# The first stage of a two-layer trunk kernel: loads in a set order, shifts by groups of 32 columns, products by arrival

## The chip, the cores and the metric

The kernel runs on one core of one Trainium2 chip. The metric is the time of one execution on the device, in microseconds (us), the median of three runs.

## The reference

The program is a backbone with two layers (DEPTH 2, D_MODEL 1024) over 256 latent tokens `x` and 256 context tokens. Each layer is a SwiGLU FFN, a token mixer with four branches, and a second FFN. Before each of the three, the activations are modulated: multiplied by 1 + scale and shifted, where shift, scale and gate come from the conditioning vector by one large product.

```python
x = x + pos_emb_2d(rows)
mod_x = (silu(c) @ w_ada[l] + b_ada[l]).reshape(..., 3, 3, D_MODEL)   # sub-layer s: shift, scale, gate
def modulate(h, mods, s):
    return h * (1 + mods[..., s, 1, :]) + mods[..., s, 0, :]
def swiglu_ffn(h, w_in, w_out):
    a = h @ w_in
    return (silu(a[..., :D_FF]) * a[..., D_FF:]) @ w_out
x = layer_norm(ALPHA * x + 0.5 * gate * swiglu_ffn(modulate(x, mod_x, 0), ...), ln_g, ln_b)
```

The context tokens take the same path with `c_ctx` in the place of `c`. All is float32. The part that the change touches is the first modulation: `shift` and `scale` of the first sub-layer for the 1024 channels, `x` with its positions, the modulated `x`, and the first products of the first FFN.

## The kernel before

**Layout.** The 256 context and 256 latent tokens stand side by side as 512 columns; the 1024 channels are eight tiles k = 0 to 7 of 128 partitions. A float32 product is made of three faster ones (`mm3`, L156): of each operand the ScalarE (ACT) makes a rounded copy `hi`, the VectorE (DVE) subtracts it to get the rest `lo` (`split`, L127), and the TensorE (PE) adds weight-hi x `xh`, weight-hi x `xl` and weight-lo x `xh`. A weight tile of 128 x 1024 (512 KB) holds 128 output channels for all eight k. It is loaded into a ring of four buffers named `raw` (`wload`, L135), split, and used in 24 products of 512 columns. In the trace all products carry the line of the helper `mm` (L122), all ACT operations that of `act` (L125), and all counted DVE operations that of `counted` (L113).

**The first stage** is `start` (L383). It goes through four groups u = 0 to 3, each with k = 2u and 2u + 1. For a group it orders on SP, the queue of the loads, two `ada` tiles (the scale columns of `w_ada`, 512 KB each, in the same `raw` ring), two tiles of `x` (`ah`) and the four shift weights `shw` of the next group.
- *Shift.* PE makes a row of 256 values from `shw` (`row`, eight products with the two columns of `ccol`), ACT copies the row, PE turns it into columns (`shift`), ACT adds the bias (`bp`).
- *Scale.* The DVE multiplies an `ada` tile with the conditioning vector, broadcast over the partitions (`cbc`), and sums: one operation of 128 x 1024 per k and vector (L421, named `junk` by its unused output). A small one adds the bias (`gp`).
- *Modulated x.* POOL (GpSimd) adds the positions (L430), ACT makes `xf` from `ah`, `gp` and `bp` and rounds it to `xh`, the DVE subtracts to `xl`.

After groups 0, 1 and 2 the function calls `mid`, which loads and splits two weight tiles of the first FFN each: six tiles, thus 6 x 24 = 144 products, that accumulate over k as the `x` tiles arrive (`mmk`).

**What sets the order.** The tile framework's scheduler orders the instructions of each engine around the program order and places the semaphores; a ring buffer is loaded again when its last reader has finished. Behind the first stage, `ffn` runs the 22 pairs of output tiles in three parts, each followed by the products of the second weight. Between tiles, `pump` (L260) takes steps from `bg`, the generators `mods` (L226): the scale, shift and gate values of the later sub-layers, by scalings of 128 x 1024 on the DVE (L235), for which one more `ada` tile is loaded into the `raw` ring every two steps.

```python
c = sp.tile([128, 2080], F32, tag="big", name=nm("cbc"), bufs=1)[:, :2 * D]
nc.sync.dma_start(c[:, q], I["cvec"][q].partition_broadcast(128))
act(hi, src, AF.Copy)
tt(out=lo, in0=src, in1=hi.bitcast(F32), op=ALU.subtract)
```

## Time and profile before

| | |
|---|---|
| median of three runs | 2256.55 us (2255.21 to 2262.13) |
| the profiled execution | 2258.55 us |
| its span in the trace | 2256.8 us |
| its mean granted PE clock | 0.993 |
| instructions in the trace | 30633 |

The span is the time from the first to the last instruction that the trace shows; the execution's own time has a little around it. The rows on which the prediction rests stand in a section of their own, below. In a row of a timeline the first number is the start in the span, the second the duration, the name before `<-` is what is written, those behind it what is read, and the brackets hold how long the engine stood idle before and what ended it. In a row of groups the part behind the first `|` is the busy time of the group and the mean of one instruction in ns, the part behind the second the idle time before them.

### The profile page before, as it was taken

The page shows a single profiled execution, that of the slowest core. Times are in us where ns is not written, and L with a number is a line of the kernel's source. Part 1 is how long each engine was busy: PE and PEld are TensorE (multiplying, and loading weights), DVE is VectorE, ACT ScalarE, POOL GpSimd, SP SyncE. Part 2 cuts the span into 40 slices and gives each one's busy share as a digit, 9 for nine tenths or more (in the row PEclk, how much of TensorE's full clock was granted, in tenths as well). Part 3 has the DMA queues.
Part 4 walks back from the last instruction along what each step waited for, and adds up shares of the span by engine and source line. Part 5 has one row for each costly group of instructions (what it writes and reads, how often), then busy time and mean ns, then how long its engine had stood idle before and what let it go on. Part 6 is the DMA issues. An engine that isn't in the chain of part 4 may idle for free.

```text
span 2256.8 us, 30633 instructions
## 1 busy us (share of the span) xinstructions
PE 2216.5 (98%) x11700; PEld 1880.7 (83%) x11700; DVE 1649.4 (73%) x2947; ACT 959.4 (43%) x1521; POOL 19.4 (1%) x82
## 2 busy tenths in 40 slices
PE   7999999999999999999999999999999999999998
PEld 4888788988888888898888888888889998998887
DVE  6998855768996754795746488766558989767777
ACT  5322223732335743362222244222326645756554
POOL 2000000000000000000000000000000000000000
PEclk9999999999999999999999999999999999999999
DMA  8676642323332132244535425554434643354652
GB/s 309 216 228 220 201 156 92 106 77 121 96 95 83 57 105 92 94 139 151 186 103 168 131 85 187 189 159 163 143 102 137 191 141 109 114 169 143 202 187 85
DMA packets 94452, 323.18 MB, mean 143 GB/s; under 512 B 10592, under 2 KB 12640, under 8 KB 94304
## 3 DMA queue, kind: packets, MB, share of 16 engines
q1 hardware_dynamic: 94304, 321.22, 44.7%
q8 instruction: 92, 1.51, 0.3%
q14 instruction: 56, 0.46, 0.1%
HBM read 320.12 MB, written 1.05 MB: 142 GB/s over the span
## 4 chain that ended last, share of the span: by engine, by line
PE 86%; DVE 6%; DMA 3%; ACT 2%; issue 2%; SPq 0%; DVEq 0%; ACTq 0%
PE mm L122 81%; DVE junk L235 2%; DVE lo L113 1%; DMA ada<-in_wada 1%; PE num L122 1%; DMA raw<-in_ffn_in 1%; DVE junk L421 1%; ACT hi L125 1%; DMA raw<-in_ffn_out 1%; DVE ah L113 1%; PE bcr L122 1%; PE gt L122 0%; PE ax L122 0%; PE qk L122 0%; PE bcm L122 0%
## 5 line engine op out<-in xcount | busy, mean ns | idle before, releaser
L125 ACT ACTIVATE hi<-raw 128x1024 fp32r<-128x1024 f32 (+1 forms) x462 | 473.2, 1030 | 996.0 <-PE mm L122 617.7
L122 PE MATMUL mm<-xh,hi 128*128 128x512 f32 (+1 forms) x2448 | 873.2, 365 | 6.7 <-ACT hi L125 3.6
L122 PE MATMUL mm<-xh,lo 128*128 128x512 f32 (+1 forms) x2448 | 849.2, 347 | 0.0
L122 PE MATMUL mm<-xl,hi 128*128 128x512 f32 (+1 forms) x2096 | 749.3, 358 | 0.4 <-DVE xl L113 0.4
L113 DVE TENSOR_TENSOR lo<-raw,hi 128x1024 fp32r<-128x1024 f32 (+1 forms) x462 | 544.8, 1184 | 234.7 <-ACT hi L125 231.2
L122 PEld LDWEIGHTS mm<-xh,hi 128*128 128x128 f32 x2448 | 460.8, 189 | 83.7 <-ACT hi L125 5.0
L122 PEld LDWEIGHTS mm<-xh,lo 128*128 128x128 f32 x2448 | 463.6, 189 | 58.6 <-DVE lo L113 0.9
L122 PEld LDWEIGHTS mm<-xl,hi 128*128 128x128 f32 x2096 | 396.0, 189 | 58.7 <-DVE xl L113 0.7
L122 PE MATMUL mm<-gh,hi 128*128 128x512 f32 (+1 forms) x1424 | 402.9, 364 | 1.8 <-ACT gh L125 1.2
L235 DVE CUSTOM_DVE_ANT_0 junk<-ada,cbc 128x1024 bf16<-128x1024 f32 x256 | 312.8, 1222 | 100.3 <-DMA ada<-in_wada 97.0
L122 PEld LDWEIGHTS mm<-gh,hi 128*128 128x128 f32 x1424 | 254.5, 188 | 50.7 <-ACT gh L125 1.6
L122 PE MATMUL mm<-gh,lo 128*128 128x512 f32 (+1 forms) x800 | 275.3, 344 | 0.7 <-DVE lo L113 0.7
L122 PEld LDWEIGHTS mm<-gh,lo 128*128 128x128 f32 x800 | 150.4, 188 | 21.4 <-DVE lo L113 1.1
L113 DVE SCALAR_TENSOR_TENSOR ah<-mm,gate,ah 128x256 f32<-128x256 f32 x216 | 95.7, 478 | 90.0 <-PE mm L122 89.6
L113 DVE SCALAR_TENSOR_TENSOR cacc<-pd,cw,cacc 128x512 f32<-128x512 f32 (+1 forms) x240 | 132.9, 609 | 0.2
L122 PE MATMUL mm<-yh,hi 128*128 128x512 f32 (+1 forms) x512 | 129.3, 339 | 0.1
L113 DVE TENSOR_TENSOR sg<-sg,mm 128x512 f32<-128x512 f32 (+1 forms) x87 | 53.6, 616 | 70.5 <-PE mm L122 70.1
L122 PEld LDWEIGHTS mm<-yh,hi 128*128 128x128 f32 x512 | 88.0, 189 | 11.6 <-ACT yh L125 0.3
L125 ACT ACTIVATE gh<-sg 128x512 fp32r<-128x512 f32 (+1 forms) x88 | 50.8, 578 | 89.5 <-DVE sg L113 89.1
L122 PE MATMUL mm<-yh,lo 128*128 128x512 f32 (+1 forms) x256 | 86.5, 338 | 0.0
L122 PE MATMUL mm<-mh,hi 128*128 128x256 f32 (+1 forms) x320 | 67.0, 306 | 0.5 <-ACT mh L125 0.3
L125 ACT ACTIVATE xf<-ah,bp,gp 128x256 f32<-128x256 f32 x88 | 48.7, 592 | 21.6 <-DVE ah L113 15.0
(263 smaller groups left out, 1798.0 us busy)
## 6 DMA issues: line engine op xcount, KB each, us to landing
raw<-in_ffn_in SPq DMA_DIRECT2D x176, 512.0 KB, 3.8
ada<-in_wada SPq DMA_DIRECT2D x136, 512.0 KB, 4.2
raw<-in_ffn_out SPq DMA_DIRECT2D x64, 512.0 KB, 3.6
raw<-in_w_G SPq DMA_DIRECT2D x64, 512.0 KB, 3.5
raw<-in_w_br SPq DMA_DIRECT2D x32, 512.0 KB, 3.5
raw<-in_ffn_out SPq DMA_DIRECT2D x32, 384.0 KB, 3.6
raw<-in_w_o SPq DMA_DIRECT2D x24, 512.0 KB, 3.5
shw<-in_wshift SPq DMA_DIRECT2D x16, 256.0 KB, 5.9
```

The costliest lines, as they stand in the source:

```text
L113: return f(*a, **k)
L122: nc.tensor.matmul(o, w, x, **kw)
L125: S.activation(o, i, f, **kw)
L235: V.tensor_tensor_reduce(out=cur["junk"], in0=w, in1=cur["c"][:, v], scale=1.0, scalar=0.0, op0=ALU.mult, op1=ALU.add, accum_out=m[:, v, t ...
L421: V.tensor_tensor_reduce(out=cur["junk"], in0=w, in1=cur["c"][:, v], scale=1.0, scalar=0.0, op0=ALU.mult, op1=ALU.add, accum_out=m[:, v, k ...
```

## The change

The first stage is written anew, in the program order that each engine is to keep: PE, SP, DVE and ACT take their instructions in the stage exactly as they are written (`manual_schedule`).
- *Loads.* `LOADS` names the order, part by part: `a` scale weights of a k, `x` a tile of x, `s` shift weights of a group, `W` a weight tile, `p` positions. Scale weights come in halves of 512 columns to blocks of the general pool (`blk`), no longer to the `raw` ring. The conditioning vector is loaded as 8 KB, and broadcast by four products on PE.
- *Shift.* The eight products of a group go to four column groups of 32 columns each (`c32`, the two columns of `ccol` and 30 of zeros); the product that makes columns of the row sums the four groups (`pick`). `SHIFTS` says after how many `mm3` of a k the next group stands on PE.
- *Group 2* also makes the scales of k = 4 and 5 on PE (`wmod`, eight blocks of 512 columns), for which the DVE has no scalings any more. The others have four half scalings each (L479).
- *Positions* are added on the DVE.
- *Products.* `TILES` says how many of the six tiles take part at each k. When a k arrives, the tiles that are new first catch up on the earlier k.
- *Behind the stage.* Loads for `mods` wait for the order of the last x load, its scalings stand behind the last `xl`; the weight tiles of j = 3 are loaded and split right behind the stage (`ahead`).

On ACT, around the `hi` of the sixth weight tile, before: `bp`, `gp` are the columns of shift and scale, `ah` the x tile (which is scaled at the end of its use), `wh` the two halves of the `hi` of the fifth and the sixth tile.

```order
L125 ACTIVATE bp_127<-shift_129,cols_99 128x2
L125 ACTIVATE xf_292<-ah_106,bp_127,gp_126 128x256 x2
L125 ACTIVATE bp_127<-shift_129,cols_99 128x2
L125 ACTIVATE xh_118<-xf_292 128x512
L125 ACTIVATE ah_106<-ah_106 128x512
L125 ACTIVATE xf_303<-ah_107,bp_127,gp_126 128x256 x2
L125 ACTIVATE wh_310<-raw_308 128x512
L125 ACTIVATE xh_120<-xf_303 128x512
L125 ACTIVATE wh_311<-raw_308 128x512
L125 ACTIVATE ah_107<-ah_107 128x512
L125 ACTIVATE wh_321<-raw_319 128x512
L125 ACTIVATE wh_322<-raw_319 128x512
```

And now (`hi_417` is the sixth tile's, `row_388` the row of group 2):

```order
L130 ACTIVATE ah_105<-ah_105 128x512
L130 ACTIVATE row_388<-row_387 128x512
L130 ACTIVATE bp_127<-shift_407,cols_99 128x2
L130 ACTIVATE gp_126<-shift_407,b_129 128x2
L130 ACTIVATE bp_127<-shift_407,cols_99 128x2
L130 ACTIVATE gp_126<-shift_407,b_129 128x2
L130 ACTIVATE hi_417<-raw_343 128x1024
L130 ACTIVATE xf_422<-ah_106,bp_127,gp_126 128x256 x2
L130 ACTIVATE xh_118<-xf_422 128x512
L130 ACTIVATE xf_458<-ah_107,bp_127,gp_126 128x256
L130 ACTIVATE ah_106<-ah_106 128x512
L130 ACTIVATE xf_458<-ah_107,bp_127,gp_126 128x256
```

The sixth tile's `hi` stood behind the `xh` of k = 4 and 5; it now stands ahead of the `xf` of k = 4, and behind the row copy and the four small operations that wait for group 2 on PE.

On the DVE, at the scalings of k = 6 and 7, before: `junk` is a scaling, the row behind it reads its sum, `alg` are small operations for later sub-layers.

```order
L421 ISA junk_98,sc_128<-ada_330,cbc_93 128x1024
L421 ISA sc_128 128x1
L113 TENSOR_SCALAR gp_126<-sc_128,cols_99 128x2
L421 ISA junk_98,sc_128<-ada_332,cbc_93 128x1024
L421 ISA sc_128 128x1
L113 TENSOR_SCALAR alg_387<-cols_100 128x8 x2
L421 ISA junk_98,sc_128<-ada_332,cbc_93 128x1024
L421 ISA sc_128 128x1
L113 TENSOR_TENSOR xl_123<-xf_352,xh_122 128x512
L113 TENSOR_SCALAR gp_126<-sc_128,cols_99 128x2
L113 TENSOR_SCALAR alg_390<-cols_100 128x8 x2
```

And now (`xl_121` is that of k = 5, `xl_123` that of k = 6, `ada_358` the scale weights of k = 7):

```order
L118 TENSOR_TENSOR xl_121<-xf_458,xh_120 128x512
L479 ISA junk_147,sc_128<-ada_353,cbc_132 128x512
L479 ISA sc_128 128x1
...
L479 ISA junk_147,sc_128<-ada_354,cbc_132 128x512
L479 ISA sc_128 128x1
L118 SCALAR_TENSOR_TENSOR gp_126<-sc_128,b_129 128x2
L118 TENSOR_TENSOR ah_108<-ah_108,pos 128x256
L118 TENSOR_TENSOR xl_123<-xf_503,xh_122 128x512
L479 ISA junk_147,sc_128<-ada_358,cbc_132 128x512
```

The scalings of k = 6 and 7 all stood ahead of the `xl` of k = 6; now those of k = 6 stand behind the `xl` of k = 5, and those of k = 7 behind the `xl` of k = 6.

```diff
-MID = (0, 1, 2)
+
+LOADS = ("a0 x0 p s0 W0 a1 x1 W1", "s1 a2 x2 W2", "a3 x3 W3", "W4 s2", "x4 x5 W5 s3 a6 x6 a7 x7")
+TILES = (1, 2, 3, 5, 6, 6, 6, 6)
+
+SHIFTS = {1: 2, 3: 8, 5: 3}
...
-    def load_c():
+    def load_c(first=False):
 
         c = sp.tile([128, 2080], F32, tag="big", name=nm("cbc"), bufs=1)[:, :2 * D]
-        for v in range(2):
-            q = slice(v * D, v * D + D)
-            nc.sync.dma_start(c[:, q], I["cvec"][q].partition_broadcast(128))
-            act(c[:, q], c[:, q], AF.Silu)
+        if first:
+            two = wp.tile([128, 1024], F32, tag="raw", name=nm("two"), bufs=4)[0:2]
+            nc.sync.dma_start(two, I["cvec"].rearrange("(v d) -> v d", v=2))
+            for v in range(2):
+                for h in range(2):
+                    p = aux("cb")
+                    mm(p, ident[0:2, v:v + 1].to_broadcast([2, 128]), two[:, h * 512:h * 512 + 512], start=True, stop=True)
+                    act(c[:, v * D + h * 512:v * D + h * 512 + 512], p, AF.Silu)
+        else:
+            for v in range(2):
+                q = slice(v * D, v * D + D)
...
+    c32 = const.tile([128, 8, 32], F32, name="c32")
+    V.memset(c32, 0.0)
+    act(c32[:, :, 0:2], ccol, AF.Silu)
+    pick = const.tile([128, 2], F32, name="pick")
+    tt(out=pick, in0=ident[:, 0:2], in1=ident[:, 32:34], op=ALU.add)
+    for j in (64, 96):
+        tt(out=pick, in0=pick, in1=ident[:, j:j + 2], op=ALU.add)
...
-            nc.sync.dma_start(w, I["wada"][l, s * 24 + t])
+            with tc.issue_after(last["dma"].ins):
+                nc.sync.dma_start(w, I["wada"][l, s * 24 + t])
             for v in range(2):
-                V.tensor_tensor_reduce(out=cur["junk"], in0=w, in1=cur["c"][:, v], scale=1.0, scalar=0.0,
-                                       op0=ALU.mult, op1=ALU.add, accum_out=m[:, v, t:t + 1])
+                with tc.issue_after(last["xl"].ins):
+                    V.tensor_tensor_reduce(out=cur["junk"], in0=w, in1=cur["c"][:, v], scale=1.0, scalar=0.0,
+                                           op0=ALU.mult, op1=ALU.add, accum_out=m[:, v, t:t + 1])
                 yield
...
-    def start(mid):
...
+    def start():
+        m = const.tile([128, 2, 2, 8], F32, name="sc00")
+        b1 = const.tile([128, 8], F32, name="b100")
+        ld, tiles, done, rows = {}, [], [], {}
+        def load(names):
+            for x in names.split():
+                n = int(x[1:] or 0)
+                if x == "p":
+                    nc.sync.dma_start(pos, I["pos"])
+                elif x[0] == "a":
+                    ld[x] = [blk("ada") for _ in range(2)]
+                    for i in range(2):
+                        nc.sync.dma_start(ld[x][i], I["wada"][0, 8 + n, :, i * 512:i * 512 + 512])
+                elif x[0] == "s":
+                    src = [I["wmod"][i] for i in range(8)] if n == 2 else [I["wshift"][min(n, 2), i] for i in range(4)]
+                    ld[x] = [blk("shw") for _ in src]
+                    for t, w in zip(ld[x], src):
+                        nc.sync.dma_start(t, w)
+                elif x[0] == "x":
+                    last["dma"] = nc.sync.dma_start(ah[n], I["xc"][n])
+                else:
+                    raw = wp.tile([128, D], F32, tag="raw", name=nm("raw"), bufs=4)
+                    nc.sync.dma_start(raw, I["ffn_in"][0, 0, n // 2, n % 2])
+                    ld[x] = raw
+        def add(n):
+            hi = wp.tile([128, 1024], F32R, tag="hi", name=nm("hi"), bufs=6)
+            lo = wp.tile([128, 1024], F32R, tag="lo", name=nm("lo"), bufs=6)
+            split(hi, lo, ld["W%d" % n])
+            tiles.append((aux() if n == 5 else mmb(), hi, lo))
+            done.append(0)
+        def products(upto):
+            for k in range(upto + 1):
+                for n in range(TILES[upto]):
+                    if done[n] == k:
+                        p, wh, wl = tiles[n]
+                        mm3(p, ktile(wh, k), ktile(wl, k), xs[k], full, k == 0, k == 7)
+                        done[n] += 1
+                        yield
+        def group(u):
+            r, rs = aux("row"), blk("row")
+            w = ld["s%d" % u]
+            n = 512 if len(w) == 8 else 256
+            for i in range(8):
+                j = 32 * (i % 4)
+                x = w[i] if n == 512 else w[i // 2][:, (i % 2) * 256:(i % 2) * 256 + 256]
+                mm(r[j:j + 32, 0:n], c32[:, i], x, start=i < 4, stop=i >= 4)
+            act(rs[:, :n], r[:, :n], AF.Copy)
+            rows[u] = rs, n
+        def columns(u):
+            rs, n = rows.pop(u)
+            q = aux("shift")
+            for i in range(n // 128):
+                mm(q[:, 2 * i:2 * i + 2], rs[:, i * 128:i * 128 + 128], pick, start=True, stop=True)
             for k in (2 * u, 2 * u + 1):
+                i = 2 * (k % 2)
+                act(b[:, k], q[:, i:i + 2], AF.Identity, bias=col(0, "b_ada", k))
+                if n > 256:
+                    act(g[:, :, k], q[:, 4 + i:6 + i], AF.Identity, bias=b1[:, k:k + 1])
+        def scales(k):
+            for v in range(2):
+                for i, w in enumerate(ld["a%d" % k]):
+                    V.tensor_tensor_reduce(out=cur["junk"][:, :512], in0=w, in1=cur["c"][:, v, i * 512:i * 512 + 512],
+                                           scale=1.0, scalar=0.0, op0=ALU.mult, op1=ALU.add, accum_out=m[:, v, i, k:k + 1])
+            stt(out=g[:, :, k], in0=m[:, :, 0, k], scalar=b1[:, k:k + 1], in1=m[:, :, 1, k], op0=ALU.add, op1=ALU.add)
+        def positions(k):
+            x3 = ah[k][:, T:].rearrange("p (r c) -> p r c", c=64)
+            pk = (pos[:, 4 * k:4 * k + 4].rearrange("p (r c) -> p r c", c=1) if k < 4 else
+                  pos[:, 16 + (k - 4) * 64:80 + (k - 4) * 64].rearrange("p (r c) -> p r c", r=1))
+            tt(out=x3, in0=x3, in1=pk.to_broadcast([128, 4, 64]), op=ALU.add)
+        def modulated(k):
+            xf = blk("xf")
+            for v in range(2):
+                act(xf[:, vcols(v)], ah[k][:, vcols(v)], AF.Identity, scale=g[:, v, k:k + 1], bias=b[:, k, v:v + 1])
+            last["xl"] = split(xs[k].hi, xs[k].lo, xf)
+        ET = mybir.EngineType
+        with tc.manual_schedule(engines={ET.PE, ET.SP, ET.DVE, ET.Activation}):
+            load_c(True)
+            nc.sync.dma_start(cols[0], I["cols"][0])
+            load(LOADS[0])
+            ts(out=b1, in0=col(0, "b_ada", 8, 8), scalar1=1.0, scalar2=None, op0=ALU.add)
+            scales(0)
+            positions(0)
+            group(0)
+            add(0)
+            columns(0)
+            modulated(0)
+            for _ in products(0):
+                pass
+            load(LOADS[1])
+            for k in range(1, 8):
+                if "a%d" % k in ld:
+                    scales(k)
+                positions(k)
+                new = list(range(TILES[k - 1], TILES[k]))
+                for n in new[:1]:
+                    add(n)
+                modulated(k)
+                for n in new[1:]:
+                    add(n)
+                if k < 4:
+                    load(LOADS[k + 1])
+                todo = products(k)
+                if k in SHIFTS:
+                    for _ in range(SHIFTS[k]):
+                        next(todo)
+                    group(k // 2 + 1)
+                    for _ in todo:
+                        pass
+                    columns(k // 2 + 1)
+                for _ in todo:
+                    pass
...
-                wh, wl = wload(I["ffn_in"][l, w, j, h])
+                wh, wl = ahead.pop((l, w, j, h), None) or wload(I["ffn_in"][l, w, j, h])
...
-                elif j == 0:
-                    mmk(tiles, xs, cs)
-                else:
+                elif j:
                     for t in tiles:
                         mmk([t], xs, cs)
+                else:
+                    for h in range(2):
+                        ahead[l, w, len(js), h] = wload(I["ffn_in"][l, w, len(js), h])
...
-    o["wshift"] = a["w_ada"][0, :, :D].reshape(4, 2, 128, 4, 256).transpose(3, 0, 2, 1, 4).reshape(4, 4, 128, 512)
+
+    w0 = a["w_ada"][0]
+    o["wshift"] = np.concatenate([w0[:, :512], w0[:, 768:D]], axis=1
+                                 ).reshape(4, 2, 128, 3, 256).transpose(3, 0, 2, 1, 4).reshape(3, 4, 128, 512)
+    o["wmod"] = np.concatenate([w0[:, 512:768], w0[:, D + 512:D + 768]], axis=1).reshape(8, 128, 512)
```

## Rows read from the trace of the kernel before

**Rows 1.** The page: busy time (share of the span) and instructions of each engine.
```profile
PE 2216.5 (98%) x11700; PEld 1880.7 (83%) x11700; DVE 1649.4 (73%) x2947; ACT 959.4 (43%) x1521; POOL 19.4 (1%) x82
```

**Rows 2.** Windows: length, PE, PEld, DVE, ACT, POOL (instructions), clock, DMA share, GB/s.
```profile
0.00:20.00 20.00, 9.32 (x36) 3.33 (x36) 7.34 (x25) 6.86 (x13) 3.29 (x12) 1.00 0.91 326
20.00:40.00 20.00, 16.14 (x65) 9.51 (x66) 16.61 (x24) 11.41 (x21) 5.68 (x4) 1.00 0.94 339
```

**Rows 3.** Chain of waits, in order of time: start, length, what.
```profile
6.03 6.44 DMA ada<-in_wada
...
76.02 2.29 DVE lo L113 x2
...
234.60 133.62 PE mm L122 x583
```

**Rows 4.** Timeline of PE: the first product, the tiles' end, and the waits.
```profile
22.37 0.50 PE L122 MATMUL mm<-xh,hi 128*128 128x512 f32 x1 [2.55 <-ACT hi L125]
...
68.11 0.39 PE L122 MATMUL ax<-xh,wl 128*128 128x512 f32 x1
68.34 0.39 PE L122 MATMUL mm<-xh,hi 128*128 128x512 f32 x1
...
131.51 0.50 PE L122 MATMUL mm<-gh,lo 128*128 128x512 f32 x1 [0.70 <-DVE lo L113]
...
233.52 0.50 PE L122 MATMUL mm<-gh,hi 128*128 128x512 f32 x1 [1.17 <-ACT gh L125]
234.60 0.50 PE L122 MATMUL mm<-gh,hi 128*128 128x512 f32 x1 [0.57 <-DVE gh L113]
```

**Rows 5.** Timeline of the DVE: the last xl of the stage.
```profile
57.18 0.69 DVE L113 TENSOR_TENSOR xl<-xf,xh 128x512 fp32r<-128x512 f32 x1
```

**Rows 6.** Groups by line and shape, whole span: busy, mean ns | idle before.
```profile
L113 DVE TENSOR_TENSOR lo<-raw,hi 128x1024 fp32r<-128x1024 f32 x422 | 513.3, 1221 | 223.4 <-ACT hi L125 219.9
...
L125 ACT ACTIVATE hi<-raw 128x1024 fp32r<-128x1024 f32 x422 | 445.3, 1060 | 917.7 <-PE mm L122 592.9 <-issue 227.2 <-DMA raw<-in_ffn_in 66.7
...
L235 DVE CUSTOM_DVE_ANT_0 junk<-ada,cbc 128x1024 bf16<-128x1024 f32 x256 | 312.8, 1222 | 100.3 <-DMA ada<-in_wada 97.0
...
L125 ACT ACTIVATE xf<-ah,bp,gp 128x256 f32<-128x256 f32 x88 | 48.7, 592 | 21.6 <-DVE ah L113 15.0 <-DVE gp L113 5.6 <-ACT ah L125 0.9
...
L113 DVE TENSOR_TENSOR ah<-ah,bcm 128x256 f32<-128x256 f32 x80 | 29.9, 409 | 1.6 <-PE bcm L122 1.6
...
L421 DVE CUSTOM_DVE_ANT_0 junk<-ada,cbc 128x1024 bf16<-128x1024 f32 x16 | 22.0, 1375 | 1.2 <-DMA ada<-in_wada 0.9
...
L113 DVE TENSOR_TENSOR xl<-xf,xh 128x512 fp32r<-128x512 f32 x8 | 5.4, 686 | 2.2 <-ACT xh L125 2.2
...
L125 ACT ACTIVATE xh<-xf 128x512 fp32r<-128x512 f32 x8 | 4.9, 620 | 0.1
...
L122 PE MATMUL st<-lns,ones 128*32 128x128 f32 x44 | 4.3, 273 | 0.0
```

**Rows 7.** DMA from 0 to 60 us, in 40 slices of 1.5 us.
```profile
GB/s 0 79 238 314 376 402 384 417 381 391 406 401 418 404 384 356 399 407 374 183 194 270 303 305 377 427 374 229 186 284 308 310 261 107 300 270 172 259 68 292
```

**Rows 8.** Window of the `mm` tiles alone: PE, PEld, DVE, ACT, clock, DMA share, GB/s.
```profile
22.00:36.10 14.10, 7.96 (x28) 4.87 (x29) 0.00 (x0) 0.00 (x0) 1.00 0.90 313
```

**Rows 9.** Timeline of PE: products with few columns of weights.
```profile
16.64 3.18 PE L122 MATMUL row<-shw,ccol 128*2 128x256 f32 x14
...
392.88 0.41 PE L122 MATMUL st<-sq,ones 128*32 128x128 f32 x4
393.12 0.39 PE L122 MATMUL st<-lns,ones 128*32 128x128 f32 x4
```

**Rows 10.** Windows behind the stage, columns as in rows 2.
```profile
57.87:131.45 73.58, 72.93 (x319) 59.36 (x317) 70.38 (x116) 19.87 (x26) 0.00 (x0) 1.00 0.69 214
131.45:234.60 103.15, 101.35 (x444) 83.00 (x444) 91.24 (x146) 31.75 (x38) 0.00 (x0) 1.00 0.72 228
```

**Rows 11.** Groups by line and shape, 0 to 60 us.
```profile
L430 POOL TENSOR_TENSOR ah<-ah,pos 128x256 f32<-128x256 f32 x8 | 11.0, 1392 | 38.0 <-DMA ah<-in_xc 38.0
```

More of the change, by code (lines that the diff above doesn't have):

```diff
@@ L105, in trunk_kernel @@
     work = {"pe": 0.0, "v": 0.0}
+    last = {}
     def size(ap):
@@ L129, in split @@
             act(hi, src, AF.Copy)
-            tt(out=lo, in0=src, in1=hi.bitcast(F32), op=ALU.subtract)
+            return tt(out=lo, in0=src, in1=hi.bitcast(F32), op=ALU.subtract)
         else:
@@ L195, in trunk_kernel @@
     cur = {}
-    def load_c():
+    def load_c(first=False):
         c = sp.tile([128, 2080], F32, tag="big", name=nm("cbc"), bufs=1)[:, :2 * D]
-        for v in range(2):
-            q = slice(v * D, v * D + D)
-            nc.sync.dma_start(c[:, q], I["cvec"][q].partition_broadcast(128))
-            act(c[:, q], c[:, q], AF.Silu)
+        if first:
[9 more added lines that the diff above has]
+                q = slice(v * D, v * D + D)
+                nc.sync.dma_start(c[:, q], I["cvec"][q].partition_broadcast(128))
+                act(c[:, q], c[:, q], AF.Silu)
         cur["c"] = c.rearrange("p (v d) -> p v d", v=2)
@@ L211, in trunk_kernel @@
         act(identr[r], ident[r, r], AF.Copy)
-    act(ccol, ccol, AF.Silu)
-    load_c()
+    c32 = const.tile([128, 8, 32], F32, name="c32")
[5 more added lines that the diff above has]
+        tt(out=pick, in0=pick, in1=ident[:, j:j + 2], op=ALU.add)
     cols = [const.tile([128, NCOL], F32, name=f"cols{l}") for l in range(DEPTH)]
@@ L437, in start @@
-        nc.sync.dma_start(masks, I["masks"].rearrange("d p t -> p d t"))
-        nc.sync.dma_start(cols[1], I["cols"][1])
+        m = const.tile([128, 2, 2, 8], F32, name="sc00")
[21 more added lines that the diff above has]
+                    ld[x] = raw
@@ L439, in start @@
+        with tc.issue_after(last["dma"].ins):
+            nc.sync.dma_start(masks, I["masks"].rearrange("d p t -> p d t"))
+            nc.sync.dma_start(cols[1], I["cols"][1])
         for k in range(8):
@@ L443, in start @@
                 a = const.tile([128, 2, 8], F32, name=f"alg{l}{s}")
-                ts(out=a[:, 0], in0=col(l, "ln_g", s * 8, 8), scalar1=ALPHA, scalar2=None, op0=ALU.mult)
-                ts(out=a[:, 1], in0=col(l, "ln_b", s * 8, 8), scalar1=ALPHA, scalar2=None, op0=ALU.mult)
+                with tc.issue_after(last["xl"].ins):
+                    ts(out=a[:, 0], in0=col(l, "ln_g", s * 8, 8), scalar1=ALPHA, scalar2=None, op0=ALU.mult)
+                    ts(out=a[:, 1], in0=col(l, "ln_b", s * 8, 8), scalar1=ALPHA, scalar2=None, op0=ALU.mult)
                 alg[l, s] = a
@@ L581, in ffn_tiles @@
             for h in range(2):
-                wh, wl = wload(I["ffn_in"][l, w, j, h])
+                wh, wl = ahead.pop((l, w, j, h), None) or wload(I["ffn_in"][l, w, j, h])
                 tiles.append((mmb(), wh, wl))
         return tiles
-    def first_tiles(n):
-        if n < 2:
-            return ffn_tiles(0, 0, (n,))
-        tiles = []
-        for h in range(2):
-            raw = wp.tile([128, D], F32, tag="raw", name=nm("raw"), bufs=4)
-            nc.sync.dma_start(raw, I["ffn_in"][0, 0, n, h])
-            hi, lo = [blk("wh", F32R) for _ in range(2)], [blk("wl", F32R) for _ in range(2)]
-            for i in range(2):
-                split(hi[i], lo[i], raw[:, i * 512:i * 512 + 512])
-            tiles.append((aux() if h else mmb(), hi, lo))
-        return tiles
+    ahead = {}
     def ffn(l, w, bd, first, cs, order, np_, nm_=1):
@@ L1247, in trunk_kernel @@
     order = (1, 0)
-    x0 = start(first_tiles)
+    x0 = start()
     bg += [mgen[0, 0], mgen[0, 1], mgen[0, 2]]
```

45 lines of the change are left out of this document (removed).

## The prediction, made before the changed kernel was run

> **What bounds the kernel now.** I read the table of busy time first: PE is busy 2216.5 of 2256.8 us [rows 1]. Only some 40 us can ever be won by removing PE's waits. The windows then say where they lie: PE is busy 9.32 us of the first 20, 16.14 of the next 20 [rows 2]. So 14.5 us, a third of all idle time, is at the start, where the change works. The chain of waits says what holds it: from 6.03 us it runs through an `ada` load, the DVE's scalings, DVE splits and the loads that these release, and only at 234.60 does it pass to PE for good [rows 3]. Up to there PE is busy but not on the chain. The PE timeline agrees: PE waits 0.70 us at 131.51 for a `lo` of the DVE, and 1.17 and 0.57 us at 233.52 and 234.60 for `gh` [rows 4]. So up to 234.6 PE has no slack against the DVE: what delays the DVE's stream by more than PE itself is delayed comes out at the end. What counts is therefore not when PE starts, but when the DVE finishes the first stage; in the kernel before it ended its last `xl` at 57.87 (57.18 + 0.69) [rows 5].
>
> **The stage, worked out.** Durations [rows 6]: a scaling holds the DVE 1.22 and 0.04 to the next, 1.26; a half one, which the trace doesn't have, is shorter by (1221 - 686) ns, the difference of a DVE split of 1024 and of 512 columns, so 0.72, four per k 2.9 us (bounds: 0.63, half a scaling, and 1.26; I take the nearest form). A split `lo` holds the DVE 1.15, `xl` 0.6, the position add on the DVE 0.41 at most (a 128x256 add), ACT `hi` 1.0, two `xf` 1.1, `xh` 0.62. PE starts a product every 0.23 us (68.11, 68.34) [rows 4].
>
> 1. First product. The first `ada` landed at 12.47 [rows 3] with 2943 KB ordered up to and with it (8, 64, 1024, 1024, 175, 136, 512). In the new order W0 ends at 2695 KB, 248 KB less at some 390 KB per us (the rate reads 356 to 418 GB/s from slice 5 to slice 19 [rows 7]): 11.8. Then `hi` 1.0, `bp`, two `xf` and `xh`: first product at 15.0 instead of 22.37 [rows 4], last split `xl0` done at 15.7. The broadcast by PE costs nothing: four products of 512 columns in the shadow of that load.
> 2. k = 1 to 3. The DVE does four half scalings (2.9), gp and positions (0.5), `lo` (beside it ACT's two `xf` and `xh`, 1.7 with hand-overs 1.9), `xl`: 5.6 us a round. In the second, `hi` stands on ACT behind the row copy and the `bp` of group 1: 2.0 more. `xl3` at 15.0 + 3 x 5.6 + 2.0 = 33.9, `lo4` done at 36.1. PE then has 31 products behind it. The kernel before had 28 at 36.1 [rows 8]: seven us of head start are spent, since a round here takes one k and the old one handled two together.
> 3. k = 4, 5. PE does 19 products (4.4) and then group 2, 16 records of 512 columns. A record of 256 took 0.227 (14 in 3.18), so 7.3 us one after another; the trace's other use of 32-column groups, `st`, has eight records of 128 columns in two groups from 392.88 to 393.51; less the 0.27 that one takes [rows 6] they start in 0.36, 0.05 apart, where half of 0.227 would be serial [rows 9]: about half. I take half, 3.6: 44.3 with a mode change of 0.2. Row copy 0.6, nine products, four `shift`, four small ACT: 47.9. ACT's order now has `hi` of the sixth tile behind these, so it ends at 48.9, `xl4` at 51.3, `xl5` at 53.7. The DVE idled 12.7 us for that `hi`.
> 4. k = 6. The DVE scales 6 at once (to 57.2), but PE must first do 10 products of tile 5 (its `lo` at 50.2), 18 of k = 4 and 9 of k = 5: 58.8. Group 3 at half 1.8, row copy beside 9 products, `shift`, `bp`: 63.8. `xf`, `xh`, `xl`: 66.3. The DVE idled 8.5.
> 5. k = 7. Its scalings stand on the DVE behind that `xl`: 2.9, gp, positions, `xf`, `xh`, `xl`: 71.9. PE's last 18 products end at 75.9, against 68.34 before.
>
> Check from PE alone: 113 products from 36.1 (25.9), groups and shifts 7.3, and waits of 6.7 (sixth tile 2.5, k = 6 2.7, k = 7 1.5) make 76.
>
> **What follows the stage.** The DVE stream behind it is the same up to the order: two `ada` scalings (2.52) were done before 57.87, now none; at the last `lo` of the first output part one scaling fewer stands before it (38 for 39), so 1.26 more to do, and the twelve small alg operations move behind the stage: 12 x 0.15 = 1.8. Shift of that `lo`: 71.9 - 57.87 + 1.26 + 1.8 = 17.1 us. Against it stands the DVE's own idle time from 57.87 to 131.45, 73.58 - 70.38 = 3.2 us [rows 10]; I let it vanish whole, as four loads lie ready when the stage ends. Shift 13.9. PE came only 0.7 too early there and is 7.6 late itself, so it waits the rest, 6.3 and the old 0.7. From 131.45 on both are shifted alike, the order is the same, and the kernel keeps the 13.9.
>
> The early loads of j = 3 save nothing: the DVE, not the loads, is late then. Homes of their own free the stage's loads from waits on the DVE: the last of them, x7, ends at 13703 KB, 11.8 + 11008 / 390 = 40.0, which is 30 us before its split, so this hides and gains nothing. POOL's adds go to the DVE, 8 x 0.41 = 3.3; it gives back 16 x (1375 - 1222) ns = 2.4, the stretching of the first stage's scalings, some of them beside POOL's adds [rows 6]; both are in the rounds. Two k less on the DVE save 4 scalings, 5.0, in the stretch where it idles: nothing.
>
> By the Trainium skill (TensorEngine Tiling (Array Packing), Tiling Modes, Key Properties) different column tiles execute in parallel, up to four of them for 32 columns; by that groups 1, 2 and 3 cost 0.9, 1.8 and 0.9 less than I take, the last `xl` comes at 68.3, the shift is 10.3 and the time 2266.9. The `st` rows have two groups and can't show four.
>
> By the Trainium skill (SBUF — State Buffer, SBUF: two separate sides) a DVE operation with two SBUF inputs and a POOL operation exclude each other for the whole instruction; the eight adds of 1.39 us [rows 11] could then have cost the DVE up to 11 us, and moving them would be worth up to 8. The scalings lost 2.4 in all, so the trace decides for that.
>
> **Sum.** The profiled execution took 2258.55 us, 2.0 above the median of the runs: 2258.55 + 13.9 = 2272.4 in a profile, 2270.4 against 2256.55. Forecast: 2270. Its own range is 2263 to 2274: shift 17.1 where no idle time vanishes, 6.7 where the three groups cost nothing (1.8, 3.6, 1.8).
>
> **Rivals.**
> - The DVE catches up. It is idle 103.15 - 91.24 = 11.9 us more from 131.45 to 234.60 [rows 10]. If its delay is absorbed there and before, PE's own delay is left: 75.9 - 68.34 = 7.6 less the 2.4 of waits that go: 2261.8, with groups that cost nothing some 5 less. For it: the idle time exists, 15 us in all. Against: it waits for loads whose buffers the DVE itself frees, so it moves with the DVE. 0.17.
> - Faster: the hand-overs of steps 3 to 5 don't cost. If PE reaches group 2 while the loads still come and each copy lies beside products, the DVE never idles its 21 us, and the last `xl` comes at 71.9 - 21.2 = 50.7. The shift is then 50.7 - 57.87 + 3.06 - 3.2 = -7.3: 2249. It decides from a last `xl` before 54.8. For it: all loads are there at 40, and PE has 33 us of products. Against: the order on ACT and DVE is fixed as listed. But my steps are sums of single durations, and the hand-overs between engines are their weakest part. 0.19.
> - The groups run one after another: 3.6 and 7.3 us, last `xl` at 80.5, shift 22.5: 2279. Against: the `st` rows. 0.08.
> - The forecast: 0.56.
>
> A measurement of this kernel tells 0.3% (6.8 us) from no change. Slower by more: the forecast less 0.02, the serial groups, and 0.02 of the first rival: 0.64. Within: 0.15 of the first rival, 0.02 of the forecast and 0.03 of the faster case, whose 2249 lies at the bound: 0.20. Faster: 0.16. The range of 2247 to 2279 leaves out the lower part of the faster case, some 0.09, and half of the serial one.
>
> **What would show it.** First product near 15 us; `xl3` near 34; a DVE gap of about 10 us that ends with the sixth tile's `hi`, one of 8 before `xl` of k = 6; the last `xl` past 66; PE waits for `lo` between 80 and 150 us; the chain of waits still on the DVE at 234. It is wrong if the last `xl` ends before 55, or if PE runs without waits from 76 to 230.

## The result and the profile after

The changed kernel took 2270.19 us (median of five runs, 2269.72 to 2275.59), the kernel before 2256.55 on the same chip: a ratio of 1.0067, 95% interval 1.0056 to 1.0078. By the medians it is slower by 13.6 us, by the means, which the ratio follows, by 15.1; the forecast was 2270. The profiled execution took 2269.72 us with a span of 2267.9 (before 2258.55 and 2256.8).

The page first (as [rows 1]), then the windows of the first 40 us (as [rows 2]):

```profile
PE 2221.2 (98%) x11712; PEld 1883.7 (83%) x11712; DVE 1646.8 (73%) x2972; ACT 961.1 (42%) x1523; POOL 8.3 (0%) x74
```
```profile
0.00:20.00 20.00, 12.84 (x33) 5.52 (x33) 10.12 (x36) 9.21 (x17) 0.54 (x10) 1.00 0.87 311
20.00:40.00 20.00, 14.77 (x55) 9.29 (x56) 14.00 (x30) 10.25 (x18) 0.00 (x0) 0.91 1.04 392
```

PE is busy longer in the first 20 us and shorter in the next 20, and the granted clock is below 1 in the second row, which it was not before. Whoever went by busy time would see a gain in these 40 us: 27.6 us of PE for 25.5. Counted by the products of the weight tiles there is none. Windows of the `mm` tiles alone (as in [rows 8]) have 43 records in 40 us before (first row) and 40 now (second row), and the 40 take longer:

```profile
0.00:40.00 40.00, 11.63 (x43) 7.52 (x43) 0.00 (x0) 0.00 (x0) 1.00 0.93 332
0.00:40.00 40.00, 15.43 (x40) 9.49 (x41) 0.00 (x0) 0.00 (x0) 0.96 0.96 352
```

Up to 26 us the changed kernel starts these products every 0.43 us, while the kernel before starts them every 0.23 us from its first ones on (23.66, 23.90, 24.12). The granted clock reads 1.00 there, but 0.43 us is also the pace of the stretches at 0.50 further down:

```profile
17.59 0.63 PE L127 MATMUL mm<-xh,lo 128*128 128x512 f32 x1
18.01 0.63 PE L127 MATMUL mm<-xh,hi 128*128 128x512 f32 x1
```

The loss shows in the DVE's timeline, which answers to [rows 5]: the split of the sixth tile, then the last three `xl`.

```profile
49.42 1.23 DVE L118 TENSOR_TENSOR lo<-raw,hi 128x1024 fp32r<-128x1024 f32 x1 [10.98 <-ACT hi L130]
...
53.42 0.69 DVE L118 TENSOR_TENSOR xl<-xf,xh 128x512 fp32r<-128x512 f32 x1 [1.33 <-ACT xh L130]
...
66.56 0.69 DVE L118 TENSOR_TENSOR xl<-xf,xh 128x512 fp32r<-128x512 f32 x1 [9.05 <-ACT xh L130]
...
72.15 0.69 DVE L118 TENSOR_TENSOR xl<-xf,xh 128x512 fp32r<-128x512 f32 x1 [1.49 <-ACT xh L130]
```

The last `xl` ends at 72.84, 15.0 us after the 57.87 of before, and the two gaps of 10.98 and 9.05 us are the 12.7 and 8.5 that were forecast. PE's timeline, in answer to [rows 4]: its first product, groups 2 and 3, the last of the 144 products, and every wait of 0.1 us or more from there to 260 us.

```profile
16.27 0.79 PE L127 MATMUL mm<-xh,hi 128*128 128x512 f32 x1 [2.14 <-ACT xh L130]
...
42.71 1.93 PE L127 MATMUL row<-shw,c 128*32 128x512 f32 x16
...
60.73 1.07 PE L127 MATMUL row<-shw,c 128*32 128x256 f32 x16
...
76.75 0.39 PE L127 MATMUL ax<-xh,lo 128*128 128x512 f32 x1
...
90.46 0.50 PE L127 MATMUL mm<-xh,hi 128*128 128x512 f32 x1 [2.44 <-ACT hi L130]
...
91.81 0.80 PE L127 MATMUL mm<-xh,lo 128*128 128x512 f32 x1 [0.61 <-DVE lo L118]
...
136.28 0.50 PE L127 MATMUL mm<-gh,lo 128*128 128x512 f32 x1 [0.17 <-DVE lo L118]
145.35 0.73 PE L127 MATMUL mm<-gh,hi 128*128 128x512 f32 x2 [0.83 <-ACT hi L130]
147.81 0.50 PE L127 MATMUL mm<-gh,lo 128*128 128x512 f32 x1 [1.73 <-DVE lo L118]
152.92 0.51 PE L127 MATMUL mm<-xh,lo 128*128 128x512 f32 x1 [0.53 <-DVE lo L118]
```

The last product starts at 76.75 for 68.11, 8.64 late; the waits behind it sum to 6.31 for the 2.44 of before. In the chain of waits PE takes over for good behind the last of them, at 152.92 and not at 234.60 [rows 3]:

```profile
152.92 230.38 PE mm L127 x1008
```

One thing was in no step of the forecast. Windows of the profile (columns as in [rows 2]) show stretches in which PE ran at a granted clock of 0.50, which is 1.2 GHz, each beginning near a wait; the kernel before has none between its first product and 392 us. Three of the four are shown, the other lies at 29.9 to 33.2 us.

```profile
50.40:53.80 3.40, 3.10 (x7) 2.49 (x8) 1.66 (x4) 3.29 (x6) 0.00 (x0) 0.50 0.49 154
...
67.40:70.80 3.40, 3.40 (x8) 2.63 (x9) 3.11 (x10) 0.44 (x1) 0.00 (x0) 0.50 0.02 5
91.30:94.70 3.40, 2.89 (x7) 2.32 (x8) 3.40 (x6) 1.06 (x1) 0.00 (x0) 0.50 0.62 207
```

Such a stretch of 3.4 us does 1.7 us of work. So, behind the stage: 8.64 + (6.31 - 2.44) + 1.7 = 14.2 us. The first norm (the `st` products, 392.88 before [rows 9]) starts at 408.00 here, 15.1 late; 0.9 us of that is in none of these terms. This is where the time is lost.

### The profile page after: what moved, and what is told of

Same layout as the page of the kernel before. It is cut to its first block, busy times and chain, and to the rows that moved or that the text cites. A ratio compares the mean times of both kernels' runs of the same rounds, so it can differ in the third digit from the quotient of the medians.

```text
span 2267.9 us, 30684 instructions
## 1 busy us (share of the span) xinstructions
PE 2221.2 (98%) x11712; PEld 1883.7 (83%) x11712; DVE 1646.8 (73%) x2972; ACT 961.1 (42%) x1523; POOL 8.3 (0%) x74
## 4 chain that ended last, share of the span: by engine, by line
PE 92%; DVE 4%; ACT 2%; DMA 1%; issue 1%; SPq 0%; ACTq 0%; DVEq 0%
PE mm L127 87%; PE num L127 1%; DVE junk L257 1%; DVE lo L118 1%; PE ax L127 1%; ACT hi L130 1%; DVE ah L118 1%; PE bcr L127 1%; DMA ah<-in_xc 1%; PE gt L127 0%; PE qk L127 0%; PE bcm L127 0%; DMA shw<-in_wmod 0%; PE C L127 0%; ACT xf L130 0%
## 5 line engine op out<-in xcount | busy, mean ns | idle before, releaser
L130 ACT ACTIVATE hi<-raw 128x1024 fp32r<-128x1024 f32 (+2 forms) x464 | 475.3, 1030 | 986.6 <-PE mm L127 617.5
L118 DVE TENSOR_TENSOR lo<-raw,hi 128x1024 fp32r<-128x1024 f32 (+2 forms) x464 | 547.2, 1184 | 244.3 <-ACT hi L130 240.9
L118 DVE SCALAR_TENSOR_TENSOR ah<-mm,gate,ah 128x256 f32<-128x256 f32 x216 | 95.6, 477 | 90.7 <-PE mm L127 90.2
```

The source lines that it names most:

```text
L118: return f(*a, **k)
L130: S.activation(o, i, f, **kw)
```

## The experiments

All are the changed kernel edited; e10 is the kernel before, edited. Each ran beside the kernel before on one chip, which was not the same chip for all, so ratios compare more safely than times. Theory A: the DVE's late stream is carried behind the stage, and PE waits for it there. B: PE's own late stage sets the end, the DVE doesn't matter. C: what stands behind the stage (early loads of j = 3, order of the background loads) costs the time. The table has, from each profiled execution, the end of the last `xl`, the start of the last of the 144 products, PE's waits from there to 260 us, the time at half clock in the same part (windows with a granted clock of 0.50), the start of the first norm; and the ratio of times with its interval.

| kernel | last xl | last product | waits | half clock | norm | ratio to before |
|---|---|---|---|---|---|---|
| before | 57.87 | 68.11 | 2.44 | 0 | 392.88 | 1 |
| changed | 72.84 | 76.75 | 6.31 | 3.4 | 408.00 | 1.0067 (1.0056 to 1.0078) |
| e1 | 70.67 | 76.22 | 5.64 | 6.8 | 407.49 | 1.0067 (1.0054 to 1.0080) |
| e2 | 68.79 | 72.71 | 6.78 | 3.4 | 404.73 | 1.0058 (1.0045 to 1.0070) |
| e3 | 70.14 | 74.07 | 6.24 | 10.2 | 407.88 | 1.0063 (1.0050 to 1.0075) |
| e4 | 86.83 | 90.66 | 6.82 | 3.4 | 422.19 | 1.0132 (1.0118 to 1.0146) |
| e5 | 72.28 | 76.12 | 8.24 | 10.2 | 409.01 | 1.0064 (1.0051 to 1.0076) |
| e6 | 52.41 | 63.38 | 3.03 | 0 | 388.59 | 0.9975 (0.9966 to 0.9985) |
| e7 | 73.65 | 77.56 | 0 | 0 | 399.04 | 1.0020 (1.0011 to 1.0029) |
| e8 | 73.47 | 77.28 | 6.73 | 6.8 | 410.35 | 1.0075 (1.0060 to 1.0090) |
| e9 | 52.14 | 63.12 | 1.36 | 0 | 386.17 | 0.9977 (0.9967 to 0.9988) |
| e10 | 58.15 | 68.57 | 0 | 0 | 390.08 | 0.9991 (0.9982 to 1.0000) |
| e11 | 74.54 | 78.47 | 6.43 | 3.4 | 409.81 | 1.0077 (1.0063 to 1.0091) |
| e12 | 72.04 | 75.97 | 0 | 0 | 397.33 | 1.0025 (1.0015 to 1.0034) |

The sum "delay of the last product, plus waits over 2.44, plus half of the half-clock time" gives the norm's shift in every row within 1.2 us, but for e5 (18.9 for 16.1), where a wait lies inside the half-clock stretch and is counted twice.

**e7: fewer background scalings behind the stage.**

```diff
-                    pump(np_)
+                    pump(np_ - (pi == 0 and bd is None))
...
-                pump(nm_)
+                pump(nm_ - (pi == 0 and bd is None))
```

> The first stage is unchanged; behind it, in the first of the three parts of the first FFN, two background scalings stand between tiles where three stood (up to 14 fewer by the end of the part; they are done in the later parts). Theory A: PE waits between 77 and 153 us (6.3 now) fall below 1, since they are waits for the DVE's stream; what stays is PE's own delay of 8.6; time 5 to 6 us less, near 2264.5, no new waits later as the DVE idles there. Theory B: PE's waits are not the DVE's backlog but half-clock stretches and loads, time within 1.5 us of 2270. Theory C: the waits are for the weight loads that the ring gives free late; then they stay, and time stays.

2260.74 us, 9.5 less than the changed kernel, though the stage ended no earlier. One row for PE from its last product to 153 us:

```profile
77.80:153.00 75.20, 75.20 (x330) 61.70 (x329) 74.16 (x123) 23.54 (x30) 0.00 (x0) 1.00 0.74 235
```

PE is busy all of it, at full clock, so B falls. The edit also takes one `ada` load out of the ring for every two scalings, so by itself it doesn't part a late DVE from late buffers (C). The trace of the changed kernel does. Its chain of waits reads, ahead of PE's last wait:

```profile
145.67 1.21 DVE junk L257
146.88 0.02 DVE mod L257
...
146.91 3.52 DMA raw<-in_ffn_in
...
150.54 1.07 ACT hi L130
...
151.64 1.24 DVE lo L118
```

PE goes on at 152.92. A background scaling that stands late on the DVE frees the buffer, the load follows, ACT rounds and the DVE splits. The DVE is busy 72.64 of the 74.92 us from the end of the stage to the `lo` for which PE waits at 147.81 (columns as in [rows 10]):

```profile
72.84:147.76 74.92, 69.19 (x291) 54.88 (x289) 72.64 (x132) 19.75 (x26) 0.00 (x0) 0.98 0.64 204
```

So the waits were the DVE's backlog, A holds, and the late loads of C are a link in its chain. The DVE is as full in e7; what changed is how many scalings stand ahead of each split. The edit gave more than the 5 to 6 us expected: the half-clock stretch (1.7) went with the waits (6.3), and the rest is open. The 2260.7 is also what the prediction's first rival gave (2261.8: PE's own delay and no more).

**e10: the same edit in the kernel before.**

> The kernel before, with two background scalings between tiles for three in the first part of the first FFN. Theory A: its three waits of PE up to 235 us (0.70, 1.17, 0.57) are waits for the DVE's stream and go; time 1 to 2.5 us less, 2253.5 to 2255. Rival (these waits are for loads): time as before within 0.7 us.

2254.57 beside 2256.20: in the profile all three waits are gone, and 1.6 us of the time, at the edge of what is measured. Even before, the DVE was what PE waited for.

**e1: the scalings of k = 6 and 7 in the DVE's gap.**

```diff
-                if "a%d" % k in ld:
+                if k < 4:
                     scales(k)
...
+                if k == 3:
+                    scales(6)
+                    scales(7)
```

> The eight half scalings of k = 6 and 7 stand behind the split of the fifth tile, where the DVE idled 10.98 us. Theory A (the DVE's late end of the stage is carried on: its last xl ended 72.84 us, 57.87 before): xl of k = 6 stays near 67, held by group 3 on PE, xl of k = 7 follows it within 2.5 us, last xl near 69.4; PE's products end as now (last starts near 76.75); PE waits between 77 and 153 us, 6.3 now, fall to 3 or 4; time 2 to 3.5 us less than the changed kernel's 2270.2. Theory B (PE's own late stage and its half-clock stretches set the end, the DVE does not): same last xl as A says, but the time unchanged within 1 us. Theory C (what stands behind the stage: early loads of j = 3, order of the background loads): unchanged.

2270.63: no change, a miss for A as I had put it. The last `xl` came 2.2 us earlier, but the DVE's timeline behind it reads:

```profile
71.47 1.22 DVE L257 CUSTOM_DVE_ANT_0 junk<-ada,cbc 128x1024 bf16<-128x1024 f32 x1
...
72.73 1.23 DVE L257 CUSTOM_DVE_ANT_0 junk<-ada,cbc 128x1024 bf16<-128x1024 f32 x1
...
74.00 1.22 DVE L257 CUSTOM_DVE_ANT_0 junk<-ada,cbc 128x1024 bf16<-128x1024 f32 x1
...
75.15 2.35 DVE L118 TENSOR_TENSOR lo<-raw,hi 128x1024 fp32r<-128x1024 f32 x2
```

The changed kernel has one scaling there and starts the two `lo` at 74.77. The scheduler put two more background scalings ahead of them, and the half-clock stretch behind the stage was twice as long (90.7 to 97.4), as was the one at 50 us inside it (49.7 to 56.4). So not the last `xl` decides, but when the splits behind it come; the last `xl` bounds that from below only.

**e2: hi and lo of the sixth tile ahead of the columns of group 2.**

```diff
-                    add(n)
+                    if n < 5:
+                        add(n)
...
                     group(k // 2 + 1)
+                    if k == 3:
+                        add(5)
```

> The hi and lo of the sixth tile stand ahead of the columns of group 2, on ACT and DVE. Theory A with step 3 of the prediction (that hi held xl of k = 4 and the sixth tile's products): lo of the sixth tile near 39 us instead of 50.6, PE has no wait of 1.75 and 0.53 us at 49.4 and 50.7, its half-clock stretch behind them goes, xl of k = 4 about 1 us earlier, group 3 on PE near 57 instead of 60.7, last xl near 69, the 144 products end 3.5 to 4 us earlier; time 3 to 4 us less, 2266.5. Theory B: the same fall, since PE's own end moves as much. Theory C: no change.

The stage moved as expected (last product 4.0 earlier, no wait at the sixth tile, no half-clock stretch there), the time by 1.7 us, 2268.45, where 3 to 4 were expected; the intervals overlap. At the norm 3.3 of the 4.0 us are still there. Step 3's hand-over is right, its worth at the end not resolved.

**e3: group 1 ahead of the products of k = 1** (`SHIFTS = {1: 0, 3: 8, 5: 3}`).

> Group 1 stands ahead of the products of k = 1 on PE, where PE waited 2.46 us for a split; nothing else moves. Theory A: the hi of the third tile on ACT no longer waits for the bias of group 1 (it ended the DVE's idle 2.79 us at 28.7), xl of k = 2 ends near 27.6 + 0.6 instead of 31.0, all behind it comes 2.8 to 3.3 us earlier, last xl near 69.5, PE's waits behind the stage stay near 6; time 2.5 to 3.5 us less, near 2267. Theory B and the rival that PE's backlog sets k = 4: k = 2 and 3 come earlier, group 2 does not, time unchanged.

The last product is 2.7 us earlier, the time the same, 2270.14. The windows say where it went:

```profile
88.70:95.50 6.80, 6.28 (x16) 4.86 (x16) 6.73 (x10) 1.06 (x1) 0.00 (x0) 0.50 0.66 205
...
146.80:150.00 3.20, 3.12 (x7) 2.48 (x8) 3.13 (x6) 0.58 (x1) 0.00 (x0) 0.50 0.91 312
```

The 10.2 us at half clock are 6.8 more than in the changed kernel, worth 3.4 us in this profile. The waits are as long as there (6.24 for 6.31), since the DVE came earlier by the same 2.7 us as PE. Why the stretches grew is not shown.

**e12: e3 and e7 together.**

> Group 1 ahead of the products of k = 1, and two background scalings between tiles for three in the first part of the first FFN. Group 1 alone brought the stage forward by 2.7 us and the time by nothing: PE waited as long for the DVE behind it and ran 10.2 us at half its granted clock for 3.4. If that is why: with the waits gone and no half-clock stretch behind the stage, the 2.7 us come through, time 2.5 us below the thinned kernel alone (2260.7), near 2258, PE's waits behind the stage under 0.5. Rival (a gain of the stage is given back later whatever the background does): 2260 to 2261.

2261.05, not below e7; a miss. In the profile the 1.6 us that the stage gained are at the norm (397.33 for 399.04) and 1.3 are left in the span (2257.6 for 2258.9), with no wait and no half-clock stretch, but the medians don't show them. Gains of 2 us are below what these runs resolve.

**e4: one column group** (the product that makes the columns then reads these 32 rows alone).

```diff
-                j = 32 * (i % 4)
+                j = 0
...
-                mm(r[j:j + 32, 0:n], c32[:, i], x, start=i < 4, stop=i >= 4)
+                mm(r[j:j + 32, 0:n], c32[:, i], x, start=i == 0, stop=i == 7)
```

> The eight products of a shift group all go to the same 32 columns, one after another. Theory A: group 2 takes 7.3 to 7.7 us instead of 1.93, group 3 3.6 instead of 1.07, groups 0 and 1 at least 1.7 more each; xl of k = 4 some 6 us later, last xl 10 to 12 us later (83 to 85), time 9 to 12 us more, near 2281. Rival (the groups lie in PE's waiting time for the DVE): groups 0 and 1 cost nothing, 2 and 3 cost what PE then lacks, time at most 4 us more.

2285.7: more than expected. Group 2 on PE:

```profile
48.45 7.05 PE L127 MATMUL row<-shw,c 128*32 128x512 f32 x16
```

7.05 us for 1.93, a factor of 3.65: the four groups do run beside each other. Group 3 took 3.64 for 1.07, group 0 5.53 and group 1 4.13 for 1.94 each (the 1.94 are at the slow pace of the first 26 us): 13.5 us more for the four. All of it lies on the path (last `xl` 14.0 later, time 15.5); none of it is hidden.

**e5: no early loads of j = 3** (the `ahead` loop left out).

> The weight tiles of j = 3 are loaded and split where every other tile is, no longer right behind the stage. Theory A (the DVE's backlog behind the stage sets PE's waits): the two splits come later in the DVE's stream, so PE meets its first wait already at the end of the 144 products, near 77 us, 1 to 3 us long, and the sum of its waits up to 155 us stays between 5 and 9; time 0 to 3 us more, 2270 to 2273. Theory C (the early loads take the ring's buffers and the DVE from the rest): time 2 us or more less.

2270.17. PE meets its first wait at 76.5, as A said, but it is 7.67 us long, up to 84.17, and not 1 to 3. A second of 0.57 follows; 8.24 us for 6.31 in sum, 10.2 us at half clock for 3.4, and the time is the same. The early loads of C neither cost nor gain while the DVE is late. The other half of C, the order of the background loads, was changed by no run.

**e8: the position adds on POOL.**

> The eight position adds are on POOL again. By the rows of before (POOL's adds 1.39 us each; scalings 1375 ns beside them, 1222 without): each add leaves the DVE 0.34 us and the half scalings that it lies beside go from 690 to 700 to 780 ns; last xl within 1.5 us of 72.8, time within 2 us of 2270. Rival (DVE and POOL exclude each other for whole instructions): half scalings beside an add take up to 1.39 us more, xl of k = 3 comes 2 to 4 us later and the time rises as much.

2272.73, 0.7 us over the bound. From the groups of the first 76 us:

```profile
L479 DVE CUSTOM_DVE_ANT_0 junk<-ada,cbc 128x512 bf16<-128x512 f32 x24 | 17.3, 720 | 4.7 <-ACT cbc L130 4.2
...
L487 POOL TENSOR_TENSOR ah<-ah,pos 128x256 f32<-128x256 f32 x8 | 6.9, 872 | 34.5 <-DMA ah<-in_xc 26.6 <-DMA pos<-in_pos 7.9
```

A half scaling takes 720 ns on the mean for 690, which is 24 x 30 ns = 0.7 us. The mean hides that nearly all take 690 as before, and two that lie beside an add take 0.29 and 0.40 us more:

```profile
24.57 0.98 DVE L479 CUSTOM_DVE_ANT_0 junk<-ada,cbc 128x512 bf16<-128x512 f32 x1
...
33.26 1.09 DVE L479 CUSTOM_DVE_ANT_0 junk<-ada,cbc 128x512 bf16<-128x512 f32 x1
```

The price of the rival didn't come: no scaling is longer by 1.39 us or near it, and `xl` of k = 3 is 0.9 us later and not 2 to 4. That the two engines hold each other up for a part of an operation fits these rows. The last `xl` moved by 0.6. A second half-clock stretch (149.7 to 153, granted 0.50) is worth 1.7 in the profile; that it makes up the rest of the 2.5 us is not shown.

**e11: the broadcast by load instead of PE** (`load_c()` for `load_c(True)`).

> The conditioning vector comes as two broadcast loads of 512 KB as in the kernel before, for 8 KB and four products on PE. Step 1 of the prediction (the loads' order in bytes sets the first product): all later loads 2.6 us later, the first product near 18 to 19 instead of 16.3; the rounds of k = 1 to 3 follow, last xl 2 to 2.5 later, time 1 to 3 us more. Rival (the four products on PE, 7.16 us in the trace, held the first row and with it the first hi): the first product is not later, 15.5 to 16.5.

2273.77. The first product came at 17.52 for 16.27: group 0 waited for its weights until 11.21, where it had stood behind the four broadcast products until 10.65. Neither side was right: the products on PE do hold the first row, and the loads of 1 MB hold it longer. The time rose by 3.6 us, where 1 to 3 were expected.

**e6: the same operations in another order.**

```diff
+                if k == 1:
+                    group(1)
...
+                if k == 3:
+                    group(2)
+                    next(todo)
+                    next(todo)
+                    columns(2)
+                    positions(4)
+                    positions(5)
+                    modulated(4)
+                    scales(6)
+                    add(5)
+                    modulated(5)
+                    for _ in range(4):
+                        next(todo)
+                    group(3)
...
+            columns(3)
+            scales(7)
+            positions(6)
+            modulated(6)
+            positions(7)
+            modulated(7)
```

> Same operations as the changed kernel in another order: group 1 ahead of the products of k = 1, group 2 ahead of those of k = 3, group 3 behind six mm3 of k = 3; xf of k = 4 and 5 as soon as group 2 is there, the scalings of k = 6 and 7 ahead of the split of the fifth x tile and of the xl of k = 6. Theory A: xl of k = 3 near 33.5, of k = 4 near 40 to 42 (now 51.7), the last xl near 50 to 54 (now 72.8, before 57.9); the DVE never idles over 4 us; the 144 products end 8 to 11 us earlier, near 66 to 68; PE's waits from there to 155 us under 2 (now 6.3); time 2252 to 2258. Theory C: the waits behind the stage stay near 6, time 2260 or more. If what the DVE gains is filled by background scalings ahead of the first splits, as in the run with the scalings moved alone, the waits fall less: 2258 to 2261.

2251.56 us: 18.6 less than the changed kernel and 4.6 less than before. The DVE's timeline: `xl` of k = 3, 4, 6 and 7.

```profile
33.17 0.69 DVE L118 TENSOR_TENSOR xl<-xf,xh 128x512 fp32r<-128x512 f32 x1 [0.35 <-ACT xh L130]
...
39.12 0.69 DVE L118 TENSOR_TENSOR xl<-xf,xh 128x512 fp32r<-128x512 f32 x1 [3.10 <-ACT xh L130]
...
49.36 0.69 DVE L118 TENSOR_TENSOR xl<-xf,xh 128x512 fp32r<-128x512 f32 x1 [1.33 <-ACT xh L130]
51.72 0.69 DVE L118 TENSOR_TENSOR xl<-xf,xh 128x512 fp32r<-128x512 f32 x1 [1.33 <-ACT xh L130]
```

The gaps of 10.98 and 9.05 us are gone, and the last `xl` ends at 52.41, below the 54.8 from which the prediction's faster rival was to decide. Its price was 2249. PE's waits, 3.03 us, are over the 2 expected, and the time lies just below the range of 2252 to 2258. So the same loads, column groups and PE scalings can be faster than the kernel before: they were not what cost the time, the order was. e6 moves the groups, the sixth tile's `hi` and the scalings together. Moved alone (e3, e2, e1) each brought the last `xl` 2.2 to 4.1 us forward and the time at most 1.7, so the share of each is not shown.

**e9: e6 with fewer background scalings (e7).**

> The order of the run before this one (e6), and in the first part of the first FFN two background scalings between tiles for three. Theory A: the DVE is no longer late, so thinning gives little, 0 to 2 us less than e6; 2251 to 2257. If the DVE's stream is still what PE waits for (background scalings put ahead of splits): 3 us or more less than e6, and below the kernel before, near 2251.

2250.94, within the noise of e6, as expected. In the profile PE's waits fall from 3.03 to 1.36 us and the norm comes 2.4 us earlier, which the medians don't resolve. Beside e10, the kernel before with the same thinning on the same chip, e9 is 3.6 us faster.

## Why the prediction was right

Its mechanism, a late DVE for which PE then waits, held from the start to the last `lo` of the first output part; behind that it did not. Several sizes were off, and they cancelled. That the time lies in the range is the mechanism; that it lies within 0.2 us of 2270 is luck.

1. **First product.** 15.0 said, 16.27 measured. "The broadcast by PE costs nothing" failed: four products took 7.16 us (from 3.56), the row of group 0 stood behind them until 10.65, and the first `hi` stood on ACT behind the copy of that row.
2. **k = 1 to 3.** The rounds took 5.58, 8.52 and 5.58 us (5.6, 7.6, 5.6 said): `xl` of k = 3 ended at 36.6 for 33.9. The terms of a round (2.9, 0.5, 1.9 and 0.6) add up to 5.9, not to the 5.6 that was carried on; that the rounds took 5.58 is luck.
3. **The groups.** I took half of the serial time, 3.6 us for group 2. It took 1.93, group 3 1.07. The rule of the Trainium skill (TensorEngine Tiling (Array Packing), Tiling Modes, Key Properties), which the prediction gave in a sentence by itself, was the better price, and e4 shows it. That the last `xl` didn't come at the 68.3 which went with it fits the late start (1.3 and 0.9 us of steps 1 and 2) and the half-clock stretch from 50.4 to 53.8, 1.7 us, ahead of group 3; these are 3.9 of the 4.5 us. No row shows the 0.2 us of a mode change: the products on both sides of group 2 start at 42.39 and 44.57, the group at 42.71, and no gap is over 0.1 us. The terms of the serial rival give a last `xl` of 79.2 and not 80.5; e4 had 86.83.
4. **The end of the stage.** Group 2 ended at 44.6 (44.3 said), the sixth tile's `hi` at 49.4 (48.9), the last `xl` at 72.84 (71.9), the last product at 77.0 (75.9).
5. **Behind it.** The last `lo` of the first output part was to come 13.9 us later: 14.0 from the stage, 3.1 of more work, less the DVE's idle time of 3.2, which was to vanish whole. It came 16.3 later (147.76 for 131.45). The stage gave 15.0 and the work 2.3 (72.64 for 70.38 us; the twelve `alg` operations took 0.96 us and not 1.8), but only 0.9 of the idle time vanished. PE stood 16.3 late there too (147.81 for 131.51): 8.64 of its own (7.6 said), 5.1 more of waits (6.3 said), 1.7 of the half-clock stretch, which was not in the sum, and 0.9 open.
6. **Wrong.** From there the shift was to be kept, with the chain on the DVE up to 234. The chain passes to PE at 152.92. One more wait of 0.53 came and the 1.17 and 0.57 us at 233 went, so the norm is 16.3 + 0.5 - 1.7 = 15.1 late. This fits a part of the first rival, that the DVE catches up where it has idle time (8.1 us from 152.92 to 235). And the quantity "last `xl`" was too simple, as e1 shows.

What stays open: in the profiled executions the lead of the kernel before falls from 15.1 us at the first norm to 11.1 in the span; the medians differ by 13.6, the means by 15.1. The profiled execution of before was 2.0 above its median. Where the other 2 went, or whether they are real, no run tells.

## What to carry to other kernels

A fixed order for in-order engines is read engine by engine: for each instruction that waits for another engine, look at what stands behind it and was ready (here eight half scalings, a weight split and two `xf` behind a row that PE hadn't yet made). The same operations were worth +13.6 us in one order and -4.6 in another. An engine with little slack behind a stage hands its delay on; thinning its background work there gave back some 9 of the 13.6 us without touching the stage.

## What the runs showed of the hardware

- A wait of PE can cost more than itself: near waits of 1.2 to 2.8 us (7.67 in e5) the granted clock fell to 0.50 for stretches of 3.4 us or more, in which products start every 0.43 us and not every 0.23. The length of the wait doesn't tell which is followed by one: a wait of 2.59 us in e2 was, one of 2.60 in e4 wasn't. It differs between executions of the same instructions too: e10 has the stage of the kernel before, and only e10 has this stretch. Each costs 1.7 us, as much as the gains in the stage that were looked for.

```profile
23.70:26.90 3.20, 3.20 (x9) 2.49 (x8) 3.17 (x4) 0.86 (x3) 3.03 (x2) 0.50 1.06 403
```
- A granted clock of 1.00 at the start of the span need not mean full pace: the changed kernel starts products every 0.43 us up to 26 us with 1.00 shown; e11 runs at the same pace there, and its granted clock reads 0.50:

```profile
18.40:28.20 9.80, 7.33 (x27) 3.80 (x28) 8.16 (x22) 3.16 (x6) 0.00 (x0) 0.50 1.04 396
```
- Eight products of 32 columns of weights in four column groups took 1.93 us, in one group 7.05 (512 columns, both at full clock).
- An add on POOL took 0.87 us beside half scalings (1.39 in the kernel before), and these 720 ns on the mean for 690; the two longest 0.98 and 1.09 us.
